# Conv pairs of 258 columns, and fixed start remainders for the rows that TensorE reads

## The chip, the cores and the metric

The kernel runs on one core of a Trainium2 chip. The metric is the device time of one execution in microseconds (us), as a median over runs. TensorE (PE) multiplies, VectorE (DVE) and ScalarE (ACT) do elementwise work, GpSimd (POOL) does some elementwise work and issues some DMAs, SyncE (SP) issues the weight loads.

## The reference, cut to what matters

One decoder layer for 512 positions behind 16 learned meta positions, width 2048, in float32:

```
h = concat(meta, x)                               # L = 528 positions
p = rmsnorm(h, g_mix) @ w_in                      # q, k, v of 8 heads; gb, gc, u of a conv group
o_attn = stick_breaking_attention(qnorm(q), knorm(k), v)
o_conv = gb * causal_dwconv3(gc * u, conv_w)      # each position needs the two before it
h = h + concat(rmsnorm(o_attn), rmsnorm(o_conv)) @ w_out
h = h + (silu(n2 @ w_gate) * (n2 @ w_up)) @ w_down,  n2 = rmsnorm(h, g_ffn)
return h[:, 16:]
```

The conv group therefore needs the 512 output positions and two more ahead of them, 514 in all.

## The kernel before, in words

Everything lies transposed: features on the 128 partitions, positions along the free dimension. A number is kept as two float32r parts, high and low, and a product of two numbers takes three matmuls: high weight by high row, high weight by low row, low weight by high row. I call these three a triple; they are the lines L734, L735, L736 in the blocked products, L275, L277, L279 in the plain ones, L834 to L836 in the output projection. A *row* here is one tile's stretch of positions that a matmul streams, and `k` counts the tiles of 128 features.

The stages, in order of time:

- **Heads** (to about 366 us): the scaled input stands in 16 pairs of tiles `nh{k}`, `nl{k}` of 528 columns each. For each head, `product` runs over k. The products `pk` and `pv` take all 528 columns in two halves of 264 (columns 0 and 264), `pq` takes the 512 columns from 16 on.
- **Two conv channel tiles by plain products** (to about 416 us): `pcu`, two halves of CH = 260 columns from column C0 = 8 on, and `pb`, 512 columns.
- **Conv pairs** (416 to 606 us): six channel tiles in pairs. `pair_product` multiplies a 2x2 block of weights by a 2x2 block of the input (upper and lower 8 tiles k, first and second half of the columns) with seven block products (Strassen-Winograd) in place of eight. Each is 8 tiles k by one triple, of width CH. There are nine pair products. The seven inputs, `conv_acts`, are: three combined blocks that lie in `blk`, three quarters of `nh`/`nl` as they are, and one combined block that is written over the second half of `nh0..7`/`nl0..7`.
- **Output projection** (to about 789 us) with rows of 512 columns in `oc`, `oc_end`, `oa`.
- **FFN** (the rest, to 2048 us) with the same `pair_product` at 256 columns; its rows lie in tiles from `slots`, each 4 + c + 60 elements long.

`form_blocks` makes the combined blocks, one k at a time, during the heads and stores them with SP into a DRAM tile `fc`. When the last head is done, GpSimd loads `blk` from `fc` with six DMAs (L693), and after the last `pb` it loads the second halves of `nh`/`nl` with 16 more (L700).

The weights come on SP's queue into `w_buf`, are split by ACT (L188) and DVE (L189) into `s_buf`, and are prepared two or three parts ahead of TensorE by `prepare`. The engines' orders follow the program's text, except where a priority is given.

Where a row begins in a partition follows from the tile sizes, 4 bytes to an element. `nh` and `nl` are 528 x 4 = 2112 bytes long, 8 x 256 + 64, and lie one behind the other: from nh to nl of the same k the start moves by 64 modulo 256 bytes, from k to k + 1 by 128. A row of `blk` is 260 x 4 = 1040 bytes, 4 x 256 + 16: from k to k + 1 the start moves by 16; from the high to the low part it moves by 8 x 1040 = 8320 bytes, 128 modulo 256. A row of the FFN's tiles is 1024 bytes and one of `oa` and `oc` 2048, so in those two stages every row of every tile begins at one remainder (240 in the FFN, 128 in the output projection, by the allocated addresses). The weights in `s_buf` all begin at remainder 128, before and after.

The functions that the change touches:

Of the kernel before, what the change touches and what calls it, by code (L numbers as in the profile page):

```python
# [9 lines left out]
F32 = mybir.dt.float32  # L10
F32R = mybir.dt.float32r
# [4 lines left out]
P = 128  # L16
# [3 lines left out]
L = META + SEQ  # L20
# [13 lines left out]
def hybrid_layer(ctx: ExitStack, tc: tile.TileContext, xT, w_in, w_out, w_gu, w_down, vecs, out):  # L34
# [9 lines left out]
    nc = tc.nc  # L44
    ve, sc, gp, pe = nc.vector, nc.scalar, nc.gpsimd, nc.tensor

    def open_pool(name, bufs=1, **kw):
        return tc.alloc_tile_pool(name=name, bufs=bufs, reuse_waits="tile", **kw)
# [3 lines left out]
    npool = open_pool("npool", side="right")  # L52
# [3 lines left out]
    atmp = open_pool("atmp", side="right")  # L56
    pp = open_pool("pp", 2, space=PSUM)
    sm = open_pool("sm", 4, space=PSUM)

    n_tmp = [0]  # L60

    def t512(cols=SEQ, tag="t", bufs=6):
        n_tmp[0] += 1
        pool = atmp if tag == "r" else tmp
        return pool.tile([P, cols], F32, tag=tag, bufs=bufs, name=f"tmp{n_tmp[0]}")
# [189 lines left out]
    def after(k_tiles, work):  # L255
        waiting.append([k_tiles, work])
# [27 lines left out]
    def product(parts, acts):  # L284
        for _ in product_steps(parts, acts, len(acts)):
            pass
# [53 lines left out]
        nc.sync.dma_start(xts[k], xT[k])  # L340

    def split_x(k):
        nh = npool.tile([P, L], F32R, tag=f"nh{k}", name=f"nh{k}")
        nl = npool.tile([P, L], F32R, tag=f"nl{k}", name=f"nl{k}")
        g = g_mix[:, k : k + 1]
        sc.activation(nh, xts[k], AF.Copy, scale=g)
        ve.scalar_tensor_tensor(nl, xts[k], g, nh.bitcast(F32), ALU.mult, ALU.subtract)
        n_hl.append((nh, nl))
# [23 lines left out]
    for a, b in FIRST:  # L372
        for k in range(a, b):
            split_x(k)
        if b == KT:
            for place in PLACES:
                load_at(place)
            limit[0] = len(ents)
        for step in steps:
            next(step)  # L380
# [22 lines left out]

    stage = open_pool("stage")
    od = {}
    C0, CH = 8, (L - 8) // 2
    fc = dram.tile([P, 4, 2, 8, CH], F32R, name="fc")

    def form_blocks(k):

        x4 = stage.tile([P, 4, CH], F32, tag="x4", name=f"x4_{k}")
        st = stage.tile([P, 8 * CH], F32R, tag="st", name=f"st4_{k}").rearrange("p (i a t) -> p i a t", i=4, a=2)
        for i, kk in ((0, k), (2, k + 8)):
            nc.sync.dma_start(x4[:, i : i + 2], two(xT[kk][:, C0:]))
        for i, kk in ((0, k), (2, k + 8)):
            sc.activation(x4[:, i : i + 2], x4[:, i : i + 2], AF.Copy, scale=g_mix[:, kk : kk + 1])
        a11, a21, a12, a22 = (x4[:, i] for i in range(4))
        ve.tensor_tensor(a22, a22, a21, ALU.subtract)
        ve.tensor_tensor(a21, a11, a21, ALU.subtract)
        ve.scalar_tensor_tensor(a11, a22, -1.0, a11, ALU.mult, ALU.subtract)  # L420
        ve.scalar_tensor_tensor(a12, a11, -1.0, a12, ALU.mult, ALU.subtract)
        split(st[:, :, 0], st[:, :, 1], x4)
        nc.sync.dma_start(fc[:, :, :, k].bitcast(F32), st.bitcast(F32))

    def stage_out(name):

        t = stage.tile([P, 8 * CH], F32R, tag="st", name=f"st_{name}")[:, : 2 * SEQ].rearrange("p (a t) -> p a t", a=2)

        def store():
            od[name] = dram.tile([P, 2, SEQ], F32R, name=f"od_{name}")  # L430
            gp.dma_start(od[name], t)

        return t[:, 0], t[:, 1], store

    def halves(ps, n):
        return ps[:, :, :n]

    def two(t):
        return t.rearrange("p (a b) -> p a b", a=2)
# [205 lines left out]
    def conv_taps(j, c1, c2, y):  # L645

        ve.tensor_tensor(c1, c1, two(r2[:, C0:]), ALU.mult)
        ve.tensor_tensor(c1, c2, c1, ALU.mult)
        cu = c1.rearrange("p a b -> p (a b)")
        o = META - 2 - C0  # L650
        sc.activation(y, cu[:, o : o + SEQ], AF.Copy, scale=cw[:, 3 * j : 3 * j + 1])
        for t in (1, 2):
            ve.scalar_tensor_tensor(
                y, cu[:, o + t : o + t + SEQ], cw[:, 3 * j + t : 3 * j + t + 1], y, ALU.mult, ALU.add
            )

    def conv_out(j, gb, y, oh, ol, s, eng=gp):
        ve.tensor_tensor(gb, gb, r[:, META:], ALU.mult)
        eng.tensor_tensor(y, y, gb, ALU.mult)
        g = g_cnv[:, j : j + 1]  # L660
        sc.activation(oh, y, AF.Copy, scale=g)
        ve.scalar_tensor_tensor(ol, y, g, oh.bitcast(F32), ALU.mult, ALU.subtract)
        square_sum(acc_c, y, j == 0, s)

    def halves_of(cols):
        return t512(2 * CH, cols, 2)[:, : 2 * CH]

    for j in range(CONV_FIRST):
        if j == 0:
            after(2, lambda: form_blocks(6))  # L670
            after(12, lambda: form_blocks(7))
        c1, c2 = halves_of("e"), halves_of("e2")
        for c in (c1, c2):
            p = pp.tile([P, 2, 512], F32, tag="pp", name="pcu")
            product([(p[:, 0, :CH], C0, C0 + CH), (p[:, 1, :CH], C0 + CH, L)], n_hl)
            sc.copy(two(c), halves(p, CH))
        y = t512(SEQ, "v", 2)[:, :SEQ]
        conv_taps(j, two(c1), two(c2), y)
        pb = pp.tile([P, 2, 512], F32, tag="pp", name=f"pb{j}")
        product([(pb[:, 0, :], META, L)], n_hl)  # L680
        gb = t512(SEQ, "e2", 2)[:, :SEQ]
        sc.copy(gb, pb[:, 0, :])
        if j == 0:
            assert not waiting
            after(10, scale_a)
            apool.release()
            atmp.release()
            const.release()
            blk_pool = open_pool("blk_pool", side="right")
            blk = blk_pool.tile([P, 3, 2, 8, CH], F32R, name="blk")  # L690
            for i, n in ((2, 3), (0, 0), (1, 2)):
                for part in range(2):
                    gp.dma_start(blk[:, i, part], fc[:, n, part], max_dma_last_dim=4160)  # L693
        oh, ol, store = stage_out(f"c{j}")
        conv_out(j, gb, y, oh, ol, t512(SEQ, "e", 2)[:, :SEQ], ve)
        store()
# [6 lines left out]
        return lambda part, k: n_hl[kk + k][part][:, a : a + CH]  # L703

    def of_blk(i):
        return lambda part, k: blk[:, i, part, k]

    conv_acts = [
        parts_of(0, C0), of_blk(2), of_blk(0), of_blk(1), parts_of(0, C0 + CH), parts_of(8, C0), parts_of(8, C0 + CH)
    ]  # L710
    stage.release()
# [131 lines left out]
    def slots(pool, dt, m, n, name, tail=60, **kw):  # L843

        c = 2 * m * n * T2
        t = pool.tile([P, 4 + c + tail], dt, name=name, **kw)
        t = t[:, 4 : 4 + c].rearrange("p (s a k t) -> p s a k t", s=m, a=2, k=n)
        return [t[:, s] for s in range(m)]

    def slot(pool, dt, n, tag, name, **kw):  # L850
        return slots(pool, dt, 1, n, name, tag=tag, **kw)[0]

    def pad(pool, n):
        pool.tile([P, n // 4], F32, name=f"pad_{pool.name}")

    acts = {}
    for i in (0, 1, 2, 5):
        acts[i] = slot(fpool, F32R, 8, f"f{i}", f"f{i}")
    pad(fpool, 160)
    fx = {i: dram.tile([P, 2, 8, T2], F32R, name=f"fx{i}") for i in (3, 4, 6)}  # L860
    def wide_tmp(tag, dt=F32, bufs=1):
# [35 lines left out]
    for i, j in enumerate(OUT_TILES):  # L897
        half, k = divmod(j, 8)
# [34 lines left out]
        if i == KT - 1:  # L933
# [9 lines left out]
            sides = fp.tile([P, 3 * T2], F32, name="sides")  # L943
            rings_p = {0: open_pool("ring_0")}
            pad(rings_p[0], 32)
            rings, n_ring, ring = {}, [6], {}

# [123 lines left out]
    with tc.high_priority(1 << 20):  # L1071
        for s in range(1, 7):
            load_acts(0, s)
    d2 = first.tile([P, 4, SEQ], F32, name="d2")
    pad(first, 11936 - 8192)
    gate(FT - 1, g1, u1, x)
    apool.release()
# [136 lines left out]
```

## Time and profile before

| what | value |
|---|---|
| median of 3 runs | 2048.35 us (2048.2 to 2049.47) |
| profiled execution | 2050.44 us, of which the span of instructions is 2048.7 us |
| granted TensorE clock | 0.998 |
| TensorE busy | 2032.3 us, 99% of the span, 16158 matmuls |
| VectorE, ScalarE, GpSimd busy | 84%, 51%, 19% |
| DMA | 361.70 MB in 161591 packets |

The profile lists groups of instructions by line and operand names, with the number of them, their busy time and the mean time of one. A matmul's shown time reaches from its start to its modelled end, and successive matmuls overlap: what a matmul costs is the distance from its start to the start of the next, which the timeline shows. A wait is idle time of an engine, given with what ended it. In the timeline each row has the start, the time, the engine, the line, the operation and what it writes and reads.

### The profile page before, as it was taken

To read this page: it belongs to the slowest core of one execution; us is meant where nothing else is said; L and a number is where in the kernel's file an instruction comes from. 1 tells how busy PE (TensorE), PEld (TensorE's weight loads), DVE (VectorE), ACT (ScalarE), POOL (GpSimd) and SP (SyncE) were. 2 spreads that over 40 slices of the span, in tenths; PEclk is the share of its full clock that TensorE was granted. 3 is DMA by queue.
4 is the path that set the end of the run, shared out by engine and by line. 5 is a ranking of instruction groups with operands and counts; after the bars stand their busy time and mean duration, and the time that the engine had idled before them with its cause. 6 is when DMAs were issued, how large, how long until landed. Compare 5 with 4: busy or idle time off the path is not lost.

```text
span 2048.7 us, 39716 instructions
## 1 busy us (share of the span) xinstructions
PE 2032.3 (99%) x16158; PEld 1969.3 (96%) x16158; DVE 1719.6 (84%) x2202; ACT 1049.3 (51%) x1517; POOL 381.7 (19%) x535
## 2 busy tenths in 40 slices
PE   9999999999999998999999999999999999999999
PEld 8999999999998888999999999999999999999999
DVE  8788878588876777998998998998998998888887
ACT  7666666344443434545545555554554544444443
POOL 0111111210015441011011111111101252223111
PEclk9999999999999999999999999999999999999999
DMA  6333343743365556555565565565555999989874
GB/s 230 102 127 120 128 134 129 255 147 103 104 213 181 182 170 221 150 168 178 150 175 150 150 175 151 154 171 158 149 176 151 280 305 311 249 237 257 229 155 88
DMA packets 161591, 361.70 MB, mean 177 GB/s; under 512 B 13568, under 2 KB 73216, under 8 KB 161408
## 3 DMA queue, kind: packets, MB, share of 16 engines
q1 hardware_dynamic: 78656, 226.10, 34.5%
q0 software_dynamic: 82752, 133.06, 24.6%
q8 instruction: 127, 2.08, 0.4%
q14 instruction: 56, 0.46, 0.1%
HBM read 278.50 MB, written 80.61 MB: 175 GB/s over the span
## 4 chain that ended last, share of the span: by engine, by line
PE 91%; DVE 4%; ACT 2%; issue 1%; DMA 1%; POOL 0%; SPq 0%; DVEq 0%; ACTq 0%; POOLq 0%
PE x L734 13%; PE x L736 13%; PE x L735 13%; PE z L734 6%; PE z L735 6%; PE z L736 6%; PE y L734 3%; PE y L735 3%; PE y L736 3%; PE po L834 3%; PE po L835 3%; PE po L836 3%; PE pv L275 1%; PE pv L277 1%; PE pv L279 1%
## 5 line engine op out<-in xcount | busy, mean ns | idle before, releaser
L188 ACT CAST s_buf<-w_buf 128x1024 fp32r<-128x1024 f32 (+2 forms) x665 | 659.3, 991 | 771.4 <-PE x L735 348.3
L189 DVE TENSOR_TENSOR s_buf<-w_buf,s_buf 128x1024 fp32r<-128x1024 f32 (+2 forms) x665 | 767.3, 1154 | 175.8 <-ACT s_buf L188 175.4
L734 PE MATMUL x<-f,s_buf 128*128 128x256 f32 x1408 | 389.5, 277 | 3.3 <-DVE u L770 2.1
L736 PE MATMUL x<-f,s_buf 128*128 128x256 f32 x1408 | 389.3, 276 | 1.8 <-DVE s_buf L189 1.8
L735 PE MATMUL x<-f,s_buf 128*128 128x256 f32 x1408 | 389.3, 276 | 0.8 <-DMA f<-fx 0.8
L197 DVE TENSOR_TENSOR w_buf<-w_buf 128x1024 f32<-128x1024 f32 (+1 forms) x243 | 277.6, 1142 | 17.9 <-DMA w_buf<-w_in 10.8
L734 PEld LDWEIGHTS x<-f,s_buf 128*128 128x128 f32 x1408 | 265.7, 189 | 4.0 <-DVE u L770 2.3
L736 PEld LDWEIGHTS x<-f,s_buf 128*128 128x128 f32 x1408 | 265.8, 189 | 2.0 <-DVE s_buf L189 2.0
L735 PEld LDWEIGHTS x<-f,s_buf 128*128 128x128 f32 x1408 | 265.9, 189 | 1.0 <-DMA f<-fx 1.0
L1019 POOL DMA_DIRECT2D fd<-s x147 | 103.7, 926 | 714.2 <-DVE s L290 698.0
L736 PE MATMUL z<-f,s_buf 128*128 128x256 f32 x704 | 193.9, 275 | 0.0
L734 PE MATMUL z<-f,s_buf 128*128 128x256 f32 x704 | 193.9, 275 | 0.0
L735 PE MATMUL z<-f,s_buf 128*128 128x256 f32 x704 | 193.9, 275 | 0.0
L736 PE MATMUL x<-ring,s_buf 128*128 128x256 f32 x608 | 167.5, 276 | 0.9 <-DVE s_buf L189 0.9
L735 PE MATMUL x<-ring,s_buf 128*128 128x256 f32 x608 | 167.4, 275 | 0.0
L734 PE MATMUL x<-ring,s_buf 128*128 128x256 f32 x608 | 167.4, 275 | 0.0
L736 PEld LDWEIGHTS z<-f,s_buf 128*128 128x128 f32 x704 | 132.2, 188 | 0.1
L735 PEld LDWEIGHTS z<-f,s_buf 128*128 128x128 f32 x704 | 132.2, 188 | 0.0
L734 PEld LDWEIGHTS z<-f,s_buf 128*128 128x128 f32 x704 | 132.2, 188 | 0.0
L1086 POOL DMA_DIRECT2D out_T<-d x62 | 60.2, 1001 | 301.9 <-DVE d L1094 241.0
L736 PEld LDWEIGHTS x<-ring,s_buf 128*128 128x128 f32 x608 | 114.2, 188 | 1.1 <-DVE s_buf L189 1.1
L734 PEld LDWEIGHTS x<-ring,s_buf 128*128 128x128 f32 x608 | 114.2, 188 | 0.0
(378 smaller groups left out, 5261.4 us busy)
## 6 DMA issues: line engine op xcount, KB each, us to landing
w_buf<-w_gu SPq DMA_DIRECT2D x176, 512.0 KB, 3.4
w_buf<-w_in SPq DMA_DIRECT2D x92, 512.0 KB, 3.4
fd<-s POOLq DMA_DIRECT2D x147, 256.0 KB, 5.3
w_buf<-w_down SPq DMA_DIRECT2D x96, 384.0 KB, 4.9
ring<-fd POOLq DMA_DIRECT2D x42, 768.0 KB, 8.8
w_buf<-w_out SPq DMA_DIRECT2D x32, 512.0 KB, 3.6
out_T<-d POOLq DMA_DIRECT2D x62, 256.0 KB, 5.5
fc<-st SPq DMA_DIRECT2D x8, 1040.0 KB, 6.3
```

What stands on the lines that cost most here:

```text
L188: sc.copy(hi, src)
L189: ve.tensor_tensor(lo, src, hi.bitcast(F32), ALU.subtract)
L197: ve.tensor_tensor(sums[name], a, b, ALU.add)
L275: pe.matmul(ps, wh, ah[:, a:b], start=k == 0, stop=False)
L734: pe.matmul(p, hi[:, kk], act(0, k), start=start and j == k == 0, stop=False, skip_group_check=skip)
L735: pe.matmul(p, hi[:, kk], act(1, k), start=False, stop=False, skip_group_check=skip)
L736: pe.matmul(p, lo[:, kk], act(0, k), start=False, stop=k == n - 1, skip_group_check=skip)
L834: pe.matmul(ps, hi[:, kk], ah, start=k == order[0], stop=False)
L835: pe.matmul(ps, hi[:, kk], al, start=False, stop=False)
L836: pe.matmul(ps, lo[:, kk], ah, start=False, stop=k == order[-1])
L1019: gp.dma_start(fd[c][s][:, :, k], t[:, :, i])
L1086: gp.dma_start(two(out[j]), c, accum_op=ALU.add)
```

## The change

Four things:

1. C0 goes from 8 to 12 and CH from 260 to 258: columns 12 to 528, still with the two positions ahead of the 512. The rows of `fc`, of `blk`, of `form_blocks` and of the conv products get two columns shorter.
2. `nh{k}` and `nl{k}` become views of one tile `n{k}` of 2 x 544 = 1088 elements: high from element 16 on, low from element 560 on. A tile is 4352 bytes, 17 x 256, so the high rows of all k begin at one remainder and the low rows at another, 128 bytes off it. By the allocated addresses the conv's rows begin at 240 (high) and 112 (low), the second halves 258 x 4 = 1032 bytes behind them at 248 and 120; `pq` and `pb` begin at 0 and 128; the halves of `pk` and `pv` at 192 and 224 (high), 64 and 96 (low).
3. `blk` becomes one tile of 8 + 48 x 288 elements with k ahead of the part: a row has a slot of 1152 bytes, 4 x 256 + 128, of which 258 elements are filled. High rows begin at 240, low ones at 112, for all k. A DMA into it now has 8 pieces of 1032 bytes on a partition where it had 2 of 4160.
4. The scratch of GpSimd's DMA descriptors in SBUF goes from the 16 KB that is the default to 8 KB on a partition, which makes room for the longer tiles.

```diff
     def split_x(k):
-        nh = npool.tile([P, L], F32R, tag=f"nh{k}", name=f"nh{k}")
-        nl = npool.tile([P, L], F32R, tag=f"nl{k}", name=f"nl{k}")
+        n = npool.tile([P, 2 * (L + 16)], F32R, tag=f"n{k}", name=f"n{k}")
+        nh, nl = n[:, 16 : 16 + L], n[:, L + 32 :]
...
-    C0, CH = 8, (L - 8) // 2
+    C0, CH = 12, (L - 12) // 2
     fc = dram.tile([P, 4, 2, 8, CH], F32R, name="fc")
...
-            blk = blk_pool.tile([P, 3, 2, 8, CH], F32R, name="blk")
+            blk = blk_pool.tile([P, 8 + 48 * 288], F32R, name="blk")
+            blk = blk[:, 4 : 4 + 48 * 288].rearrange("p (i k a t) -> p i k a t", i=3, k=8, a=2)
+            pad(blk_pool, 128)
             for i, n in ((2, 3), (0, 0), (1, 2)):
                 for part in range(2):
-                    gp.dma_start(blk[:, i, part], fc[:, n, part], max_dma_last_dim=4160)
+                    gp.dma_start(blk[:, i, :, part, :CH], fc[:, n, part])
...
-        return lambda part, k: blk[:, i, part, k]
+        return lambda part, k: blk[:, i, k, part, :CH]
...
-    nc = bacc.Bacc("TRN2", target_bir_lowering=False, num_devices=1)
+    nc = bacc.Bacc("TRN2", target_bir_lowering=False, num_devices=1, dynamic_dma_scratch_size=8192)
```

(`pad`, an unused tile that shifts what is allocated behind it, is moved up in the text.)

No engine's order changes: each has as many instructions as before, in the same sequence. What differs is widths and places. On TensorE, where the conv pairs first read `blk` (`z` is a PSUM bank, `nh`, `nl`, `n` the input's parts), it was

```order
1797 L734 MATMUL x_4699<-nh_246,s_buf 128x260
1798 L735 MATMUL x_4699<-nl_247,s_buf 128x260
1799 L736 MATMUL x_4699<-nh_246,s_buf 128x260
1800 L734 MATMUL z_4698<-blk,s_buf 128x260
1801 L735 MATMUL z_4698<-blk,s_buf 128x260
1802 L736 MATMUL z_4698<-blk,s_buf 128x260
```

and is now, at the same place in the row of instructions,

```order
1797 L739 MATMUL x_4684<-n_239,s_buf 128x258
1798 L740 MATMUL x_4684<-n_239,s_buf 128x258
1799 L741 MATMUL x_4684<-n_239,s_buf 128x258
1800 L739 MATMUL z_4683<-blk,s_buf 128x258
1801 L740 MATMUL z_4683<-blk,s_buf 128x258
1802 L741 MATMUL z_4683<-blk,s_buf 128x258
```

The lines move by five and the last dimension by two columns; nothing else. On GpSimd, at the loads of `blk` and of the input's second halves, it was

```order
115 L309 TENSOR_TENSOR acc_a<-acc_a,tmp_4321 128x512
116 L693 DMA blk<-fc 128x2x1040 x6
117 L431 DMA od_c_4361<-st_c_4354 128x1024
118 L700 DMA nl_171<-fc 128x260
119 L700 DMA nh_170<-fc 128x260
```

and is now

```order
115 L312 TENSOR_TENSOR acc_a<-acc_a,tmp_4305 128x512
116 L698 DMA blk<-fc 128x8x258 x6
117 L434 DMA od_c_4346<-st_c_4339 128x1024
118 L705 DMA n_170<-fc 128x258 x2
119 L705 DMA n_173<-fc 128x258 x2
```

The DMAs stand at the same places; those into `blk` are cut into more pieces, and the two loads of one k now go into one tile.

More of the change, by code (lines that the diff above doesn't have):

```diff
@@ L58, in hybrid_layer, with pad @@
     sm = open_pool("sm", 4, space=PSUM)
+    def pad(pool, n):
+        pool.tile([P, n // 4], F32, name=f"pad_{pool.name}")
     n_tmp = [0]
@@ L851, in slot @@
         return slots(pool, dt, 1, n, name, tag=tag, **kw)[0]
-    def pad(pool, n):
-        pool.tile([P, n // 4], F32, name=f"pad_{pool.name}")
     acts = {}
```

## The prediction

> **What bounds the kernel now.** I read the page's busy times first, then its chain, then the same stretches of three stages side by side, and last single starts in the timeline.
>
> ```profile
> span 2048.7 us, 39716 instructions
> PE 2032.3 (99%) x16158; PEld 1969.3 (96%) x16158; DVE 1719.6 (84%) x2202; ACT 1049.3 (51%) x1517; POOL 381.7 (19%) x535
> PE 91%; DVE 4%; ACT 2%; issue 1%; DMA 1%; POOL 0%; SPq 0%; DVEq 0%; ACTq 0%; POOLq 0%
> ```
>
> TensorE works through 99% of the span and is 91% of the chain that ended last. What it waited for while the conv pairs ran (416 to 606 us) is all in these two rows:
>
> ```profile
> PE x L734 <- ACT sides_c L764: 0.5, 2, 0.3
> PE x L736 <- DVE s_buf L189: 0.2, 1, 0.2
> ```
>
> So there is 0.7 us to be had from waits there; the rest is the matmuls themselves. The next rows give three stretches without a long stall, in the conv pairs, the FFN and the output projection (columns: stretch, length, then busy time and count of PE, PEld, DVE, ACT, POOL, the granted clock, DMA share and rate):
>
> ```profile
> 436.50:487.00 50.50, 50.50 (x424) 50.50 (x423) 42.23 (x47) 24.19 (x34) 1.78 (x1) 1.00 0.32 105
> 1000.00:1050.00 50.00, 50.00 (x444) 50.00 (x443) 43.96 (x50) 25.01 (x35) 6.34 (x9) 1.00 0.53 153
> 641.00:691.00 50.00, 50.00 (x222) 41.43 (x221) 35.16 (x48) 19.01 (x30) 22.40 (x25) 1.00 0.59 179
> ```
>
> All three run at the full clock with TensorE always busy. The price of a matmul is the distance between starts. For that I take two far rows of the timeline each: 33 steps of 256 columns in the FFN, 33 of 260 in the conv pairs, 27 of 512 in the output projection, 11 of 512 in `pq`, 22 of 264 in `pk` (two to a row).
>
> ```profile
> 999.76 0.28 PE L736 MATMUL z<-f,s_buf 128*128 128x256 f32 x1
> ...
> 1003.50 0.28 PE L736 MATMUL x<-f,s_buf 128*128 128x256 f32 x1
> ```
> ```profile
> 464.05 0.28 PE L736 MATMUL x<-blk,s_buf 128*128 128x260 f32 x1
> ...
> 468.00 0.29 PE L736 MATMUL z<-blk,s_buf 128*128 128x260 f32 x1
> ```
> ```profile
> 699.73 0.39 PE L834 MATMUL po<-oa,s_buf 128*128 128x512 f32 x1
> ...
> 705.85 0.39 PE L834 MATMUL po<-oc,s_buf 128*128 128x512 f32 x1
> ```
> ```profile
> 99.90 0.41 PE L275 MATMUL pk<-nh,s_buf 128*128 128x264 f32 x2
> 100.14 0.40 PE L277 MATMUL pk<-nl,s_buf 128*128 128x264 f32 x2
> 100.39 0.40 PE L279 MATMUL pk<-nh,s_buf 128*128 128x264 f32 x2
> ...
> 102.56 0.40 PE L279 MATMUL pk<-nh,s_buf 128*128 128x264 f32 x2
> 102.80 0.39 PE L275 MATMUL pq<-nh,s_buf 128*128 128x512 f32 x1
> ...
> 105.34 0.40 PE L279 MATMUL pq<-nh,s_buf 128*128 128x512 f32 x1
> ```
>
> FFN: 3.74 us / 33 = 113.3 ns at 256 columns. Output projection: 6.12 / 27 = 226.7 ns at 512. That is 0.443 ns a column with nothing on top, and these are the two stages whose rows all begin at one remainder modulo 256 bytes. By that line 260 columns are worth 115.1 ns, 264 are 116.9. Measured: conv pairs 3.95 / 33 = 119.7 ns (4.6 over the line), `pk` 2.66 / 22 = 120.9 ns (4.0 over), `pq` 2.54 / 11 = 230.9 ns (4.2 over). Here the start's remainder moves from row to row. I call this surplus, about 4 ns a matmul at any of the three widths, the premium. What causes it the trace does not say: start steps and odd widths go together at 260 and 264, but `pq` has the output projection's width and pays too, so width alone is not it.
>
> **The change part by part.** Counts come from these groups (line, engine, operation, count, busy us and mean ns of one):
>
> ```profile
> L735 PE MATMUL x<-nl,s_buf 128*128 128x260 f32 x216 | 61.1, 283 | 0.0
> L735 PE MATMUL z<-blk,s_buf 128*128 128x260 f32 x144 | 40.6, 282 | 0.0
> L735 PE MATMUL x<-blk,s_buf 128*128 128x260 f32 x72 | 20.3, 282 | 0.0
> L735 PE MATMUL y<-nl,s_buf 128*128 128x260 f32 x72 | 20.4, 284 | 0.0
> L277 PE MATMUL pcu<-nl,s_buf 128*128 128x260 f32 x128 | 25.8, 283 | 0.0
> L277 PE MATMUL pk<-nl,s_buf 128*128 128x264 f32 x256 | 52.3, 286 | 0.0
> L277 PE MATMUL pq<-nl,s_buf 128*128 128x512 f32 x128 | 50.5, 395 | 0.0
> L277 PE MATMUL pb<-nl,s_buf 128*128 128x512 f32 x32 | 12.5, 391 | 0.0
> ```
>
> Each is one line of a triple, so three times as many: conv pairs 3 x 504 = 1512, `pcu` 384, `pk` and with it `pv` 1536, `pq` 384 and `pb` 96, together 480.
>
> 1. *Two columns less.* 1512 + 384 = 1896 matmuls x 2 x 0.443 ns = 1.7 us, all on TensorE's path. The elementwise work of the conv gets 2 columns in 260 shorter; it lies beside TensorE (DVE is at 42.23 of 50.50 us in the stretch above) and is worth nothing.
> 2. *Rows of the conv pairs at fixed remainders.* Before, no start in a triple followed one with the same remainder (steps of 128, 128, 16 in `blk`; 64, 192, 128 in `nh`/`nl`). After, the steps are 128, 128 and 0: from high to low, from low to high, and from high to the next tile's high. Ends of the range: if premium needs a step, a third to all of it goes; if the width of 258 keeps it up, none. The nearest rows for a step of 128 are those of `blk`, which pay 4.6 ns on average with two such steps in three; the nearest for a step of 0 are FFN and output projection, which pay none. I take a third: 504 x 4.6 = 2.3 us, bounds 0 and 1512 x 4.6 = 7.0 us (with `pcu` 8.7 us). `pcu` alternates its two halves, has no step of 0 and gets nothing in the sum.
> 3. *`pq` and `pb`.* Steps were 64, 192, 128, and become 128, 128, 0. A third of 480 x 4.2: 0.7 us, bounds 0 and 2.0.
> 4. *`pk` and `pv`.* The halves of 264 columns step by 32, then by 96 and so on; before there were such steps too, and none is 0 now. I take 0. Bounds: the whole premium, 1536 x 4.0 = 6.1 us of gain, and a loss (first rival below).
> 5. *The loads of `blk`* are cut from 1536 pieces of 4160 bytes into 6144 of 1032.
>
> ```profile
> 381.82 4.35 POOL L693 DMA_DIRECT2D blk<-fc  x6 [0.30 <-POOL acc_a L309]
> ...
> 405.77 0.54 POOL L700 DMA_DIRECT2D nl<-fc  x1 [17.90 <-PE pb L279]
> DMA to landing us min/median/max: 5.7/13.2/21.1
> q0 software_dynamic: 82752, 133.06, 24.6%
> 421.66 0.28 PE L734 MATMUL z<-blk,s_buf 128*128 128x260 f32 x1
> ...
> 430.28 0.28 PE L734 MATMUL x<-nh,s_buf 128*128 128x260 f32 x1
> ```
>
> They are issued from 381.8 us and first read at 421.7: 39.8 us of cover, of which at most 24.7 are used (4.35 us of issue, 21.1 to land; the last issue starts before 386.2, so by 407.3). A packet of this queue took 0.246 x 16 x 2048.7 / 82752 = 97 ns of one engine on average, at 133.06 MB / 82752 = 1608 bytes. At that price 6144 of them take 6144 x 97 / 16 = 37 us, an upper bound since they are shorter. Just covered, so nothing. Behind them in the queue stand the 16 loads of the second halves (L700), read from 430.3 us on; if the cover is gone, they come last (see the rivals). GpSimd, busy 19%, may need some us more to issue; behind it stands only the store of `od_c`, which is read only for the output projection.
>
> 6. *The scratch* holds half the descriptors. If GpSimd must wait for room, it waits between 382 and 420 us, where it has those loads alone; the trace shows no wait of that kind. Nothing, by the same cover. *One tile for both parts* and *the moved pads* leave the engines' orders as they are: nothing.
>
> Sum: 1.7 + 2.3 + 0.7 = 4.7 us. The profiled execution took 2050.44 us, its span 2048.7, the 1.7 us around it stay; it becomes 2045.7. It stands 2.1 us above the median of the three runs, 2048.35, and that median becomes 2043.7. A change of 0.2%, 4.1 us, is about what a measurement of this kernel can tell from none.
>
> **Rivals.**
>
> *The premium goes altogether.* For: it is absent in both stages in which each row begins as the last one did, and after the change every triple repeats the one before, which no stage with a premium does now; a regular pattern of two remainders might serve as well as one. Against: two steps in three are still 128 bytes, and `blk` pays now with such steps. It gives 1.7 + 8.7 + 6.1 + 2.0 = 18.5 us: 2029.9. Between this and the forecast everything is possible, for instance that it goes in the conv pairs alone (1.7 + 7.0: 2039.7).
>
> *Only the columns count*, or not even they: the premium belongs to widths that are no multiple of 64 columns, or to any step. 258 is such a width, and 8.7 of the 16.8 us of premium are paid at 260. Against it stands `pq`. It gives 2048.35 - 1.7 = 2046.7.
> The Trainium skill's page "TensorE: Matmul & The Clock Gate", section "Back-to-back issue gap", gives N/2.4 + 2.5 ns from start to start for N columns on the warm clock, with no word of where the row begins. By that rule the layout is worth nothing and two columns 0.83 ns, 1.6 us over the 1896 matmuls: this rival. The trace departs from it: 113.3 ns where it gives 109.2, 226.7 where it gives 215.8, and at 260 columns 119.7 where it gives 110.8; it knows no premium, so I give it no more than the rows do.
>
> *Slower: the repetition locks at a dear phase.* Now the premium varies from triple to triple and is paid as an average; with fixed remainders each triple pays the same. In `pk` above, two matmuls from 100.14 to 100.39 us take 0.25 us, 125 ns each, the average being 120.9. If the halves of `pk` and `pv` lock there, that is 1536 x 4.1 = 6.3 us lost against 1.7 us of columns, the conv unchanged: 2053.0. It decides from 124.7 ns on: (4.1 + 1.7) / 1536 = 3.8 ns over the average.
>
> *The loads come late.* If `blk` takes its 37 us, it lands at 418.8, and the 2048 packets of the second halves, 2048 x 97 / 16 = 12.4 us, at 431.2, after the first read at 430.3; with the weight loads on the same engines it may be some 3 us late. That eats most of the forecast gain: 2046.7.
>
> **How the numbers follow.** The premium goes altogether or nearly (to 2036): 0.25. The forecast, a part of it (2037 to 2045.5): 0.36, of which 0.04 lies above 2044.25, the bound of a tellable gain. Columns only: 0.21. Dear phase: 0.13. Late loads: 0.05, of which 0.02 slower. Faster by over 0.2%: 0.25 + 0.32 = 0.57. Within: 0.04 + 0.21 + 0.03 = 0.28. Slower: 0.15. The likeliest is the forecast, 2043.7. The range reaches down to 2029, to take in the first rival, and up to 2050, which leaves out the dear phase and little else.
>
> **What would show it.** The distance between starts in the conv pairs: 117.3 ns (119.7 less 0.9 for the columns less 1.5 for a third of the premium) would bear out the forecast, 114.2 the first rival, 118.8 or more the second. `pq` at 229.5 or so, `pk` unchanged at 120.9; either at its line (226.7, 116.9) speaks for the first rival, `pk` above 124 for the dear phase. The FFN and the output projection should keep 113.3 and 226.7. A wait of TensorE on `blk` near 420 us or on `n` near 430 us would show the loads late. I am wrong if the premium hangs on something that the layout leaves alone, or if it goes as a whole when the pattern repeats.

## The result, and the profile after

The changed kernel took 2059.2 us (median of 6 runs, 2056.76 to 2061.34), the kernel before 2049.35 on the same chip (6 runs, 2048.2 to 2050.99): 1.0049 times as long, 95% interval 1.0039 to 1.0059, some 10 us slower. I had forecast 2043.7 and a range to 2050. The profiled execution took 2061.34 us, its span 2059.6, at the same granted clock, 0.998.

The first two lines of the page, to lay beside those of before (2048.7; PE 2032.3, DVE 1719.6):

```profile
span 2059.6 us, 39716 instructions
PE 2036.8 (99%) x16158; PEld 1968.7 (96%) x16158; DVE 1719.9 (84%) x2202; ACT 1050.4 (51%) x1517; POOL 384.2 (19%) x535
```

The span has grown by 10.9 us. TensorE is busy 4.5 us more and idle 6.4 us more: it waits for something that it did not wait for before. To find where, I laid TensorE's instructions of the two traces side by side, in order. The loss is gathered in many small steps between 120 and 446 us; from then on the distance stays near 12 us, to within a microsecond. The one transfer that runs once a head through that time shows it in a row. These are the groups of `fc`'s stores, of before and of after (columns: shortest, median and longest time of the issue in ns, then the start of the first and of the last):

```profile
L423 SPq DMA_DIRECT2D fc<-st x8: 525/525/599, 96.3 to 365.7; - x8
```
```profile
L426 SPq DMA_DIRECT2D fc<-st x8: 524/525/597, 95.3 to 376.5; - x8
```

The first store starts 1.0 us earlier after the change, the last 10.8 us later. The waits between 120 and 392 us say what grew. Before (engine, tile and line that waited, what ended the wait, then us in total, times, longest):

```profile
POOL lw L570 <- ACT bh L289: 10.5, 6, 2.1
...
DVE spl L290 <- ACT sph L289: 5.2, 13, 0.9
...
ACT x L416 <- DMA x<-xT: 2.0, 4, 0.8
...
PE c L582 <- ACT sph L289: 0.3, 1, 0.3
PE c L583 <- DVE spl L290: 0.2, 1, 0.2
```

and after:

```profile
POOL lw L573 <- ACT bh L292: 21.8, 6, 5.2
...
DVE spl L293 <- ACT sph L292: 16.5, 13, 4.1
ACT x L419 <- DMA x<-xT: 14.2, 6, 4.0
...
PE ss_k L463 <- ACT sh_k L292: 1.9, 2, 1.0
...
PE c L586 <- DVE spl L293: 1.7, 6, 0.6
...
PE c L585 <- ACT sph L292: 1.5, 2, 1.2
PE ss_k L464 <- DVE sl_k L293: 1.1, 3, 0.4
```

Read from the third line: ScalarE waits 14.2 us, where it waited 2.0, for the loads `x<-xT` at the head of `form_blocks`. Behind that wait, in ScalarE's order of instructions, stand its splits for the attention (`sph`, `bh`, `sh_k`); for these wait VectorE and GpSimd (11 us more each), and at the end TensorE, on `c` and `ss_k`, some 6 us by these rows. Counted from the distances between starts, where a stall is a distance more than 16 ns over the line, TensorE loses 20.8 us in stalls between 120 and 395 us, and 10.2 before.

Why are the loads of x late? The transfers, grouped (count, KB of each, median us from issue to landing), before and after:

```profile
fc<-st SPq DMA_DIRECT2D x8, 1040.0 KB, 6.3
...
x<-xT SPq DMA_DIRECT2D x16, 260.0 KB, 6.0
```
```profile
fc<-st SPq DMA_DIRECT2D x8, 1032.0 KB, 7.5
...
x<-xT SPq DMA_DIRECT2D x16, 258.0 KB, 7.3
```

The store of `fc` got smaller and takes longer. It stands on SP's queue just ahead of the loads of x of the next `form_blocks`. One by one, the eight stores landed after these times (us; the packets are the 8192 of the eight stores, one to a row, 1024 to a store, worked out from the trace's records of them):

| kernel | landings of the eight stores | mean | packet ns, median / 99th percentile |
|---|---|---|---|
| before: rows of 1040 bytes, 1040 apart | 6.57 6.35 6.28 6.24 6.44 5.89 6.32 5.86 | 6.24 | 48 / 95 |
| after: rows of 1032 bytes, 1032 apart | 6.95 9.35 8.08 6.99 6.72 9.56 8.97 6.81 | 7.93 | 48 / 344 |

The typical packet is as fast as before; one in a hundred takes seven times as long as that or more. So the suspect stood before the first experiment: rows of `fc` in DRAM that begin every 1032 bytes.

The distances between matmul starts, for which the change was made, moved little. Four pairs of rows of the timeline: 69 steps of `z<-blk`, `x<-blk` and `z<-blk` in the first pair product, the same 69 steps in the second, 11 of `pq`, 33 of the FFN.

```profile
432.42 0.28 PE L739 MATMUL z<-blk,s_buf 128*128 128x258 f32 x1
...
440.39 0.28 PE L739 MATMUL z<-blk,s_buf 128*128 128x258 f32 x1
...
451.03 0.28 PE L739 MATMUL z<-blk,s_buf 128*128 128x258 f32 x1
...
459.31 0.29 PE L739 MATMUL z<-blk,s_buf 128*128 128x258 f32 x1
```
```profile
101.85 0.40 PE L278 MATMUL pq<-n,s_buf 128*128 128x512 f32 x1
...
104.38 0.39 PE L282 MATMUL pq<-n,s_buf 128*128 128x512 f32 x1
```
```profile
1003.00 0.28 PE L741 MATMUL y<-f,s_buf 128*128 128x256 f32 x1
...
1006.74 0.28 PE L741 MATMUL x<-f,s_buf 128*128 128x256 f32 x1
```

FFN 3.74 / 33 = 113.3 ns, as before. `pq` 2.53 / 11 = 230.0. And the rows of `blk`: 7.97 / 69 = 115.5 ns in the first pair product, 8.28 / 69 = 120.0 in the second, from the same tile, at the same addresses and the same width. So the premium is not a fixed price of where a row begins; the same rows run with it or almost without it.

Both speeds are patterns that repeat. In the first the single distances go 115, 115, 117 ns, one triple after the other; in the second, on `blk`, 119, 117, 121, 124, 117, 122, every two triples. The first holds for the first five block products of the stage, whose rows begin at 240 and 112. The change comes in the sixth, the first whose rows begin at 248 and 120, and the 57 products behind it average 120 each, on the input as on `blk`, to the end of the conv pairs; whether the new start brings it about was not tried. Here are 48 steps on the input in the middle of the stage, rows at 240 and 112 and then at 248 and 120, 5.76 / 48 = 120.0 ns:

```profile
503.39 0.28 PE L739 MATMUL y<-n,s_buf 128*128 128x258 f32 x1
...
509.15 0.28 PE L739 MATMUL x<-n,s_buf 128*128 128x258 f32 x1
```

The runs below that keep these rows and only move `fc` or the x loads show the same two speeds, with the change at the same product.

Averages over all distances without a stall (ns; in brackets over the line of 0.443 ns a column):

| rows | before | after |
|---|---|---|
| conv and `pcu` on the input | 119.8 at 260 (4.7) | 120.2 at 258 (6.0) |
| conv on `blk` | 119.8 at 260 (4.7) | 119.5 at 258 (5.3) |
| `pk`, `pv`, 264 | 120.7 (3.8) | 122.0 (5.1) |
| `pq`, `pb`, 512 | 230.5 (3.8) | 229.8 (3.1) |
| FFN 256; `oa` 512 | 113.4; 226.7 (0) | 113.4; 226.7 (0) |

### The profile page after: what moved, and what is told of

It reads as the page before. It is cut to its first block, busy times and chain, and to the rows that moved or that the text cites. A ratio compares the mean times of both kernels' runs of the same rounds, so it can differ in the third digit from the quotient of the medians.

```text
span 2059.6 us, 39716 instructions
## 1 busy us (share of the span) xinstructions
PE 2036.8 (99%) x16158; PEld 1968.7 (96%) x16158; DVE 1719.9 (84%) x2202; ACT 1050.4 (51%) x1517; POOL 384.2 (19%) x535
## 4 chain that ended last, share of the span: by engine, by line
PE 67%; DVE 2%; ACT 1%; issue 0%; DMA 0%; DVEq 0%; ACTq 0%
PE x L739 11%; PE x L740 11%; PE x L741 11%; PE z L740 6%; PE z L739 6%; PE z L741 6%; PE y L740 3%; PE y L741 3%; PE y L739 3%; PE po L841 3%; PE po L839 3%; PE po L840 3%; DVE s_buf L192 1%; DMA w_buf<-w_gu 0%; ACT s_buf L191 0%
```

## Experiments

### Whose is the loss: the store or the layout?

Theory A: the store of `fc`, whose rows begin every 1032 bytes, and the x loads behind it. Theory B: the layout, with its finer loads and small scratch. Four kernels on one chip, with the kernel before at 2048.6 us.

**Rows of `fc` 1088 bytes apart**, on the changed kernel:

```diff
-    fc = dram.tile([P, 4, 2, 8, CH], F32R, name="fc")
+    fc = dram.tile([P, 4, 2, 8, 272], F32R, name="fc")[:, :, :, :, :CH]
```

> The changed kernel, with each row of fc in DRAM given a slot of 272 elements (1088 bytes, 17 x 64) of which 258 are filled; all else as it is. Theory A, the store's rows: rows of 1032 bytes that lie one behind the other make the store of fc land in 6.7 to 9.6 us (before: 5.9 to 6.6), the x loads of the next form_blocks stand behind it on SP's queue, and 10 us are lost by 446 us. If it is where the rows begin that matters, the landings go back to about 6.3 us and the time to 2049 to 2051. If it is the length of 1032 bytes, landings stay near 8 us and the time at 2059. Theory B, the layout (the start remainders, the finer loads of blk): landings may change, the time stays at 2058 to 2060.

The group of the stores, the two transfers, and ScalarE's wait between 120 and 395 us:

```profile
L426 SPq DMA_DIRECT2D fc<-st x8: 524/525/597, 95.0 to 365.5; - x8
```
```profile
fc<-st SPq DMA_DIRECT2D x8, 1032.0 KB, 6.1
...
x<-xT SPq DMA_DIRECT2D x16, 258.0 KB, 6.2
```
```profile
ACT x L419 <- DMA x<-xT: 2.5, 4, 1.0
```

2048.7 us, 1.0000 of before (0.9991 to 1.0008). The rows are as short and as many as in the changed kernel, only their place in DRAM differs, and the whole loss is gone: the last store starts at 365.5 us again, TensorE's stalls between 120 and 395 us are 10.0 us. So theory A holds, by the place of the rows and not by their length.

**Two columns less, and nothing else**, on the kernel before:

```diff
-    C0, CH = 8, (L - 8) // 2
+    C0, CH = 12, (L - 12) // 2
...
-                    gp.dma_start(blk[:, i, part], fc[:, n, part], max_dma_last_dim=4160)
+                    gp.dma_start(blk[:, i, part], fc[:, n, part], max_dma_last_dim=4128)
```

> The kernel before with 258 columns (C0 = 12, CH = 258; the loads of blk in pieces of 4128 bytes, two to a partition); the layout of nh, nl and blk and the scratch as before. Theory A: the store of fc lands in 7 to 9.5 us, ScalarE waits for the x loads some 8 us or more in all between 120 and 390 us (before 2.0), and the time is 8 to 10 us over before, 2057 to 2060. Theory B: no slower than before, 2047 to 2049.

The stores and ScalarE's wait again:

```profile
L423 SPq DMA_DIRECT2D fc<-st x8: 524/525/598, 95.0 to 375.7; - x8
```
```profile
ACT x L416 <- DMA x<-xT: 14.4, 6, 3.5
```

2059.66 us, 1.0054 of before (1.004 to 1.0068): the change's whole loss, from the part of it that I had put down as a sure gain. It shows the columns' price too, since the layout is that of before: `blk` at 258 columns takes 120.1 ns where it took 119.8 at 260, the rows of the input 120.1 where they took 119.8. Narrower by 0.9 ns by the line, each matmul got longer by 0.3.

**The layout alone**, on the changed kernel:

```diff
-    C0, CH = 12, (L - 12) // 2
+    C0, CH = 8, (L - 8) // 2
```

> The changed kernel with 260 columns (C0 = 8, CH = 260): fixed remainders, finer loads and the small scratch stay, rows of fc are 1040 bytes again. Theory A: landings near 6.3 us, ScalarE's wait for x near 2 us, and what the layout alone is worth, which by the distances between matmul starts is between nothing and 2 us lost: 2048 to 2052. Theory B: 2057 to 2061.

The same two rows:

```profile
L426 SPq DMA_DIRECT2D fc<-st x8: 524/525/598, 95.3 to 365.5; - x8
```
```profile
ACT x L419 <- DMA x<-xT: 2.1, 4, 1.0
```

2051.49 us, 1.0014 (1.0005 to 1.0023): no stalls, but 2.9 us (1.0 to 4.7) slower than before. The distances say where: 122.0 against 120.7 ns in `pk` and `pv`, 120.9 against 119.8 on the input, 122.1 against 119.8 on `blk`, 229.7 against 230.5 in `pq`; 1536 x 1.3 + 1248 x 1.1 + 648 x 2.3 - 480 x 0.8 = 4.5 us by averages, within the interval. At 260 columns the fixed remainders do not pay, they cost. The two columns count differently here: the run with 1088 bytes between rows has the same layout at 258 columns and took 2048.7 us on the same chip, 2.8 us less (1.0 to 4.5, from the runs of both). By averages, 648 x 2.6 + 1248 x 0.7 = 2.6 us. So columns and layout do not simply add up: narrower rows gained on the new layout and not on the old one.

**The x loads ahead of the store**, on the changed kernel: `form_blocks` k issues the loads of k + 1 before its own store.

```diff
+        if k < 7:
+            load_x4(k + 1)
         nc.sync.dma_start(fc[:, :, :, k].bitcast(F32), st.bitcast(F32))
```

> The changed kernel with the two x loads of form_blocks k + 1 put on SP's queue just ahead of the store of fc of form_blocks k, instead of behind it. If what costs is that the x loads stand behind the slow store: ScalarE's wait for x goes (under 1 us in all), the store still lands in 7 to 9.5 us, the time goes to 2048 to 2051. If the slow store costs by holding up other transfers or what ScalarE's split waits for (the free st buffer): 2056 or more. Theory B: unchanged, 2058 to 2060.

The stores, and the two transfers:

```profile
L435 SPq DMA_DIRECT2D fc<-st x8: 524/525/599, 96.2 to 364.5; - x8
```
```profile
fc<-st SPq DMA_DIRECT2D x8, 1032.0 KB, 8.8
...
x<-xT SPq DMA_DIRECT2D x16, 258.0 KB, 4.5
```

2048.87 us, 1.0000 (0.9991 to 1.0008). The store is as slow as ever (6.4 to 10.0 us, now from behind the x loads), x lands in 4.5 us, ScalarE's wait for it is gone from the list, and so is the loss. That closes the chain: what cost 10 us was not the slow store but the loads that stood behind it on the queue.

The same edit on the kernel before:

> The kernel before (260 columns, old layout) with only the x loads of form_blocks k + 1 put ahead of the store of fc of k. ScalarE's wait for x was 2.0 us in all there and little of it reached TensorE: 0 to 1.5 us gained, 2047 to 2048.6 us. If the later store collides with other transfers: 2049 or more.

2047.33 us, 0.9995 (0.9986 to 1.0004): as expected, and too small to tell from nothing.

### What about the place of a row in DRAM?

Two slots between 1032 and 1088 bytes, one run of each:

```diff
-    fc = dram.tile([P, 4, 2, 8, CH], F32R, name="fc")
+    fc = dram.tile([P, 4, 2, 8, 260], F32R, name="fc")[:, :, :, :, :CH]     # the other: 262
```

> The changed kernel with a slot of 260 elements (1040 bytes) for each row of fc, 258 filled: every row begins at a multiple of 16 bytes. If it is the start at an odd multiple of 8 bytes that slows the store: landings of 5.9 to 6.6 us as before, and about 2049 us. If rows need a start at a multiple of 64 bytes or a full slot: 7 to 9.5 us and about 2059.

> The changed kernel with a slot of 262 elements (1048 bytes) for each row of fc, 258 filled: every second row begins at an odd multiple of 8 bytes, and no two rows share a piece of 16 bytes. If it is the start that matters: landings of 7 to 9.5 us and about 2059 us, as in the changed kernel. If it is two rows in one piece of 16 bytes: 5.9 to 6.6 us, about 2049.

The kernel before took 2048.6 and 2049.0 us on the chips of these two runs.

| rows of 1032 bytes, apart by | landings of the eight stores (us) | mean | packet 99th percentile | time |
|---|---|---|---|---|
| 1032 (after) | 6.95 9.35 8.08 6.99 6.72 9.56 8.97 6.81 | 7.93 | 344 ns | 2059.2 |
| 1040 | 6.28 7.24 6.07 7.66 6.57 7.42 6.12 7.95 | 6.91 | 266 ns | 2052.48 |
| 1048 | 5.90 6.13 7.61 7.76 6.29 6.61 7.44 7.26 | 6.88 | 244 ns | 2053.11 |
| 1088 | 5.99 6.03 6.34 6.20 6.85 6.09 6.17 5.85 | 6.19 | 99 ns | 2048.7 |

None of the four outcomes that were written down came: both lie in the middle. Starts at multiples of 16 bytes do not cure it, starts at odd multiples of 8 do not make it worse than that. A gap of 8 or 16 bytes behind each row takes away some 60% of the loss per store, one of 56 bytes all of it; yet rows of 1040 bytes without any gap are fast too (6.24 us, before). So neither the gap nor the start alone decides, and what does stays open. The Trainium skill's page "DMA: Bandwidth & Descriptors", section "Specifications", gives 512 bytes as the least transfer for full rate, below which the DMA does a read-modify-write; all rows here are twice that, so its rule does not cover this loss.

### What is the premium?

The prediction took it as the price of a start at another remainder than the row before. The next kernels all have the x loads ahead of the store.

**256 of the 258 columns** (the first matmul of an accumulation keeps all 258; the kernel leaves out the last two columns of each half):

```diff
+                c = slice(0, w if start and j == k == 0 else min(w, 256))
-                pe.matmul(p, hi[:, kk], act(0, k), ...)
+                pe.matmul(p[:, c], hi[:, kk], act(0, k)[:, c], ...)
...
```

> The changed kernel with the x loads ahead of the store, and in the conv pairs every matmul but the first of an accumulation streams 256 of the 258 columns (the last two columns of each half are left out, so this computes less). Starts are as after: 240, 112, 240 in each triple. Theory S, the premium comes with a start at another remainder than the last: the two steps of 128 in a triple still cost, 113.4 + 2/3 x 4.6 = 116.4 ns from start to start, 2043 to 2044 us. Theory W, it comes with a width that is no multiple of 64 columns: 113.4 ns as in the FFN, and 1512 x 6.5 ns less, 2039 us.

69 steps of `blk` in the second pair product:

```profile
438.24 0.28 PE L751 MATMUL z<-blk,s_buf 128*128 128x256 f32 x1
...
446.68 0.28 PE L751 MATMUL z<-blk,s_buf 128*128 128x256 f32 x1
```

2049.24 us, 1.0004 of before (0.9995 to 1.0013). 8.44 / 69 = 122.3 ns; over the stage, all distances under 200 ns taken, 119.3 on the input and 122.3 on `blk`. Neither number came. The FFN's width alone does not help: on `blk`, with two columns less to stream, a matmul takes longer than at 258 (119.5 in the changed kernel). The starts are those of the changed kernel, 240, 112, 240, so this does not show steps of 128 to be free; it shows that theory S had their price wrong.

**One remainder for high and low**, all steps 0:

```diff
-        n = npool.tile([P, 2 * (L + 16)], F32R, tag=f"n{k}", name=f"n{k}")
-        nh, nl = n[:, 16 : 16 + L], n[:, L + 32 :]
+        n = npool.tile([P, 1152], F32R, tag=f"n{k}", name=f"n{k}")
+        nh, nl = n[:, 16 : 16 + L], n[:, 592 : 592 + L]
```

> The changed kernel with the x loads ahead of the store, and n's tiles 1152 elements long with the low row at element 592: high and low rows of all k begin at one remainder; scratch 4 KB to make room. All steps in pq, pb, pcu and in the conv products on n are 0. Theory S: pq goes from 229.8 to 226.7 ns, the conv products on n from 120.2 to 114.3 ns, blk stays near 119.5; 480 x 3.1 + 1248 x 5.9 ns less, 2040 us. Theory W: pq to 226.7 at most, the conv stays at 119 to 120; 2047 to 2049 us.

From the timeline, 11 steps of `pq`, then 69 steps of `blk` in the first and in the second pair product:

```profile
105.30 0.39 PE L278 MATMUL pq<-n,s_buf 128*128 128x512 f32 x1
...
107.86 0.39 PE L282 MATMUL pq<-n,s_buf 128*128 128x512 f32 x1
...
421.43 0.28 PE L748 MATMUL z<-blk,s_buf 128*128 128x258 f32 x1
...
429.41 0.28 PE L748 MATMUL z<-blk,s_buf 128*128 128x258 f32 x1
...
438.93 0.28 PE L748 MATMUL z<-blk,s_buf 128*128 128x258 f32 x1
...
447.21 0.28 PE L748 MATMUL z<-blk,s_buf 128*128 128x258 f32 x1
```

2046.46 us, 0.999 (0.9981 to 0.9999). `pq`, now without any step, got dearer: 2.56 / 11 = 232.7 ns (232.4 on average, 229.8 with steps). The rows of `blk`, whose steps did not change, got cheaper, 116.4 on average: 7.98 / 69 = 115.7 in the first pair product, 8.28 / 69 = 120.0 in the second, and near 116 again in later ones. The same two speeds as in the changed kernel, in another mixture.

**Rows of `blk` 1024 bytes apart**, with 256 columns of each (the last two are left out again):

```diff
-            blk = blk_pool.tile([P, 8 + 48 * 288], F32R, name="blk")
+            blk_t = blk_pool.tile([P, 8 + 48 * 256], F32R, name="blk")
```

> As the run that streams 256 of 258 columns, and the rows of blk stand 1024 bytes apart instead of 1152, start remainder modulo 256 bytes 240 for all (256 columns of each are loaded; the last two columns of each half are left out). Now every step in blk is a multiple of 1024 bytes, as in the FFN and the output projection. Theory M, a row is free if it begins where the last one began modulo 1024 (or 512) bytes: blk from 120.0 to 113.4 ns, n unchanged near 119.4; 648 x 6.6 = 4.3 us less than there, 2045 us. Theory O, the premium belongs to the conv stage for another reason (its transfers, other engines, where the tiles lie): blk stays at 117 to 121, 2049 us.

23 and then 46 steps of `blk` in the timeline:

```profile
420.32 0.28 PE L755 MATMUL z<-blk,s_buf 128*128 128x256 f32 x1
...
422.98 0.28 PE L753 MATMUL x<-blk,s_buf 128*128 128x256 f32 x1
...
428.19 0.28 PE L755 MATMUL z<-blk,s_buf 128*128 128x256 f32 x1
```

2044.12 us, 0.9977 (0.9967 to 0.9986). 2.66 / 23 = 115.7 ns in the first block product after the input's rows, 5.21 / 46 = 113.3 in the next two, the FFN's price; 114.3 on average, against 122.3 in the run that streams 256 columns from rows 1152 bytes apart; 648 x 8.0 = 5.2 us by that, and the ratios differ by 0.0027, 5.5 us. It is theory M's number, and the next run takes modulo 1024 away as its reason. What is left as the likeliest is that all rows of `blk` now begin at one remainder modulo 256, worth the whole premium at this width; the next run was made on rows of 512 columns, not on `blk`.

**Gaps between the rows of the output projection**, on the kernel before with the x loads first:

```diff
-        t = pool.tile([P, 2 * n * SEQ], F32R, name=name)
-        return t.rearrange("p (h a t) -> p h a t", h=n, a=2)
+        t = pool.tile([P, 2 * n * (SEQ + gap)], F32R, name=name)      # gap: 64 in oa, 128 in oc and oc_end
+        return t.rearrange("p (h a t) -> p h a t", h=n, a=2)[:, :, :, :SEQ]
```

> The kernel before with the x loads ahead of the store, scratch 4 KB, and gaps between the 512-column rows of the output projection: rows of oa stand 2304 bytes apart (one remainder modulo 256, steps of 256, 768 and 512 modulo 1024), those of oc and oc_end 2560 bytes apart (one remainder modulo 512, steps of 512 modulo 1024). Theory R, one remainder modulo 256 is enough, as the prediction had it: all stay at 226.7 ns; 2047 to 2048 us. Theory M with 512: oc stays, oa goes to 229 to 232; with 1024: both go there; 384 to 768 matmuls x 3 to 5 ns, 1 to 4 us more. Theory O: all stay.

23 steps of `oa`:

```profile
609.07 0.39 PE L843 MATMUL po<-oa,s_buf 128*128 128x512 f32 x1
...
614.28 0.39 PE L845 MATMUL po<-oa,s_buf 128*128 128x512 f32 x1
```

5.21 / 23 = 226.5 ns; `oc` and `oa` average 226.7 both (2046.69 us, 0.999, 0.998 to 0.9999). One remainder modulo 256 does suffice here, 1024 is not needed. But these rows step by 2304 and 4608 bytes, just as `pq` did in the run with one remainder, where it took 232.4. What differs is where the rows begin: at 128 here, at 0 there.

**The same, 128 bytes later:**

```diff
-        nh, nl = n[:, 16 : 16 + L], n[:, 592 : 592 + L]
+        nh, nl = n[:, 48 : 48 + L], n[:, 624 : 624 + L]
```

> As the run with one remainder for the high and the low rows of n, but all of them 128 bytes later in their tiles: the rows of pq and pb begin at remainder 128 modulo 256 (there 0), those of pcu and of the conv products on n at 112 and 120 (there 240 and 248), with the same steps. The rows of oa in the run with gaps had the same steps, began at 128 and took 226.7 ns; pq began at 0 and took 232.4. If the start remainder itself decides: pq goes to 226.7 ns, 480 x 5.7 = 2.7 us less than there, 2043 to 2045 us. If the stage does (other work beside it, or the place of the tiles): pq stays at 229 to 232, 2046 to 2047 us. For 258 columns no theory is left that says more than that they stay at 116 to 121.

Two times 11 steps of one `pq`, ahead of and behind a group of the attention's matmuls:

```profile
101.67 0.40 PE L278 MATMUL pq<-n,s_buf 128*128 128x512 f32 x1
...
104.20 0.39 PE L282 MATMUL pq<-n,s_buf 128*128 128x512 f32 x1
...
105.08 0.39 PE L278 MATMUL pq<-n,s_buf 128*128 128x512 f32 x1
...
107.58 0.39 PE L282 MATMUL pq<-n,s_buf 128*128 128x512 f32 x1
```

2044.8 us, 0.998 (0.9971 to 0.9989): the fastest kernel of the study that computes everything, about 4 us ahead of before. The first eleven steps of this `pq`, which follow the rows of `pk`, take 2.53 / 11 = 230.0 ns, those after the attention's matmuls 2.50 / 11 = 227.3, and within them the surplus runs out: from 101.67 us on, single distances lie up to 9 ns over the line, after about seven matmuls they lie on it, to within 1 ns, and stay there. In the run with starts at 0 they go on varying, up to 14 ns over the line, to the end of each group. On average `pq` and `pb` take 228.7, between the two outcomes that were written down. The runs with starts at 0 and at 128 differ in the program only by these 128 bytes, so the start decides whether the surplus dies out; `pk` and `pv` got cheaper as well (120.4 against 122.0), the conv did not (119.6 on the input, 117.4 on `blk`).

Taken together: rows came down to the line where all of them begin at one remainder modulo 256 and are 256 or 512 columns wide (the FFN, `oc` and `oa`, `oa` with gaps, `blk` at 1024 bytes, `pq` at 128). 256 columns without one remainder did not do it (122.3), nor one remainder with 258 columns (119.4 on the input). `pq` at 0 has both and stays at 232, so a third condition is missing. This is read off the runs after the fact; no run was made to test it.

## Why the prediction was wrong, point by point

- **The step that failed** is the first of the change part by part, "Two columns less". It priced the matmuls, put the elementwise work at nothing, and has no term for the store. Two columns also move every row of `fc` in DRAM: I followed the loads from `fc` (step 5) and never the store into it, which is on SP's queue, in the profile and in the diff's own line `fc = dram.tile([P, 4, 2, 8, CH])`. The trace of before showed ScalarE waiting 2.0 us in all for the x loads behind that store, so these loads had no slack; with 1.7 us more on each landing the wait became 14.2 us. Against the kernel before on the same chip the changed kernel takes 1.0049 of the time, with 1088 bytes between the rows of `fc` 1.0000: the place of the rows is the whole loss, some 10 us.
- **Its own term** depended on the layout: 1.7 us of gain expected; on the old layout 1896 matmuls got longer by 0.3 ns, 0.6 us of loss by averages, on the new one the columns gained 2.8 us.
- **Steps 2 and 3** took a third of the premium as the price of steps. The premium is not a fixed price per step: the same `blk` rows, with the same steps, ran at 115.5 and 120.0 ns within one trace. What the terms came to: 120.2 and 119.5 ns in the conv where 117.3 was forecast; for `pq` 229.8 against a forecast of 229.5, near enough, for a reason that did not hold (with no step at all it took 232.4).
- **The premise behind both**, that the FFN and the output projection pay nothing because their rows begin at one remainder modulo 256, was half right: one remainder took the premium off `blk` at 256 columns (122.3 to 114.3) and the gaps in `oa` left it at 226.7, but it was not sufficient for `pq` at 0 or for rows of 258 columns, the width of this change.
- **Step 4**, nothing for `pk` and `pv`: 1.3 ns more each, 1536 x 1.3 = 2.0 us of loss by averages, inside the bounds given and on the side of the dear phase (the third rival, where the step says the first), far from that rival's 125 ns.
- **Steps 5 and 6** held: the loads of `blk` land in a median of 15.8 us where they took 13.2, and TensorE's one wait between 395 and 470 us, 1.4 us, is for a weight (`s_buf`) and not for `blk` or `n`. The small scratch shows nowhere. The cover that step 5 says is used, 24.7 us, is 25.5 by its own rows (407.3 - 381.8); nothing hangs on it.
- **The rivals.** "Only the columns count" comes nearest to what the layout was worth, about nothing; "a dear phase" has the right kind of mechanism, a pattern that repeats and stays, but not its place or price: it came in the conv pairs, which that rival left unchanged, at 120.0 ns, only 0.2 over the average before. None of them was a store.
- **The reckoning**: 2059.2 - 2043.7 = 15.5 us of miss. 9.85 are the loss against the kernel before, all of it the place of the rows in DRAM; 4.65 are the gain that did not come, as layout and columns together are worth 0.0 (-1.8 to 1.6, the changed kernel with the wide slots against before); and 1.00 is the median before, 2049.35 in six runs where the forecast started from 2048.35 in three.

## What to carry to other kernels

When a size changes, follow every access that has it as a stride, stores to DRAM among them, and look at what stands behind each of these on its queue; the cheapest cure here was the order on the queue, loads that somebody waits for ahead of a store that nobody does. Look at where rows of a DRAM buffer begin and end: 56 unused bytes behind each were worth 10 us here. And do not read a surplus per matmul off an average as a price per address before two passes over the same tile have been compared.

## What the runs showed that I had not expected

- A store of 1 MB in 1024 rows took 7.9 us with rows of 1032 bytes 1032 apart and 6.2 with the same rows 1088 apart; the median packet was 48 ns in the former and in the kernel before alike, the 99th percentile 344 against 95.
- Matmuls on the same tile, with the same addresses and the same width, run at two speeds, 115.5 and 120.0 ns at 258 columns. Each is a repeating pattern of distances; in the changed kernel the rows ran at the first for some 120 matmuls and then at the second for over a thousand.
- With one start remainder of 128, rows of 512 columns settle to 226.7 ns within about seven matmuls of a disturbance; with one remainder of 0 they stay near 232. Rows of 256 columns settle at 240, `blk` at 1024 bytes within about ten. Why 128 and 240 do and 0 does not stays open (the weights, which all begin at 128, may have to do with it), and so does what sets which of its two speeds a row of 258 takes.
